# Decayed reads made one head pair ahead, and the norm moved behind the masks, in a bidirectional RWKV-7 kernel

## The chip, the cores and the metric

The kernel runs on one core of a Trainium2 chip. The metric is device time in microseconds, the median of several runs. The engines are PE (TensorE, matmuls), DVE (VectorE), ACT (ScalarE), POOL (GpSimd) and SP (SyncE, which here only issues DMAs). Each engine works through a queue of its own in a fixed order, and waits at an instruction until the semaphores that it needs have been raised.

## What is computed

One layer of a bidirectional RWKV-7 mixer beside a short gated convolution, for 128 context and 256 latent tokens, D = 2048, 32 heads of 64 channels. The input projection `z = h @ w_in` feeds both branches. The first branch is a recurrence in each direction:

```python
def step(S, inp):
    r_t, w_t, k_t, v_t, a_t, b_t = inp
    sa = jnp.einsum('dbhij,dbhj->dbhi', S, a_t)
    S = S * w_t[..., None, :] + sa[..., :, None] * b_t[..., None, :] + v_t[..., :, None] * k_t[..., None, :]
    y = jnp.einsum('dbhij,dbhj->dbhi', S, r_t)
    return S, y
...
y = ys[0] + ys[1]
mu = jnp.mean(y, axis=-1, keepdims=True)
var = jnp.mean(jnp.square(y - mu), axis=-1, keepdims=True)
y = ((y - mu) * lax.rsqrt(var + GN_EPS)).reshape(bsz, t, D_A) * lnx_g + lnx_b
...
y_a = (y.astype(h.dtype) * jax.nn.silu(g_a)) @ w_out_a
...
y_b = (b_gate * u * jax.nn.silu(g_b)) @ w_out_b
merged = jax.nn.sigmoid(m_a) * y_a + jax.nn.sigmoid(m_b) * y_b
return merged @ w_o, S_fin
```

The outputs are the residual streams after a final norm and the final states of the context tokens.

## The kernel before

All data is fp32. A large matmul is made of three passes over operands that are split into a high and a low part (`mm3`, L80 to L83; the split L85 to L89 is a cast on ACT, line L88, and a subtraction on DVE, line L89). Three such matmuls of 128x384 are called a dense step here. The projections are a stream of dense steps (class `Stream`, L111 to L180). The stream loads its weights (`raw`), splits them (`whi`, `wlo`) and is moved on by `ds_.go(n)`: n steps are written into PE's queue at that place. It has an order of fills: rk and gv of the next pair first, then gates (bc, bx, bg, gb, ma, mb), and at the end ob, the output projection of the convolution branch.

The recurrence is worked in chunks of 64 tokens (six, two of context and four of latent tokens) for a pair of heads, in a loop over 16 pairs b (L973 to L1002). One iteration consists of these parts, in the order in which they are written, and PE executes them in this order, with dense steps in between:

- `prep_b` makes the decayed operands: `pr` (kk and r times the decay, the "decayed reads") and `bk` (the keys). Then come 14 dense steps (`PB0`), the transposes of the last pair's normed output (`finish`, py L948), and the masked products pA of direction 0, 6 steps (`PB1`) and of direction 1 (24 small matmuls each, L708). DVE masks them into `A` (L714), SP brings the 32x32 blocks through DRAM into another layout (`ui` L719, `un` L732, `ux` L734), and DVE inverts the triangular systems in 30 short steps (L740, L742), beginning with an add on the diagonal (L745). The result goes back through `uo` and is transposed ("turned").
- `prep_c` brings the transposed v into `sav` by eight POOL DMAs (L777) and transposes the keys (pb L784).
- `prep_a` and `prep_k` make the decay, keys and rates of pair b+1; `prep_k` is called at the fourth step of the scan.
- `scan` runs two chains, 0 over the context chunks and 1 over the latent ones, both directions at once. A chunk is po (reads from the state, L816), an add into sav (L817), pq (L833), a copy, pu (L840), and the new state st (L845). When both chains are done, py2 (L910, 24 small matmuls) makes the outputs and DVE adds them to ytok (L913).
- `norm` (L927 to L942) does mean, variance and scaling of ytok on DVE, with the square on ACT and the power `rs` on POOL (L941).

The order of PE's queue is the order of writing. The orders of the other engines are set by a scheduler at compile time, by priorities: what is written in the scan is raised by 300, and otherwise what is written earlier comes earlier. The function `load_yb` (L511) is called when the stream reaches the first step of ob0. It reads the convolution branch's 16 tiles back from DRAM (`yst_b`, SP), casts them (`ybh`, L508, ACT) and subtracts (`ybl`, L509, DVE).

Of the kernel before, what the change touches and what calls it, by code (L numbers as in the profile page):

```python
# [56 lines left out]
def hybrid_step(ctx, tc, cst, x_prompt, x_sample, state_f, state_b, c, c_ctx, ada_w, ada_b, norm_g,  # L57
# [614 lines left out]
    def prep_b(b, o):  # L672

        r, kk = r_[b], o["kk"]
        o["pr"], o["bk"] = [], []
        for d in range(2):
            ep, em, kd, bn = o["ep"][d], o["em"][d], o["kd"][d], o["bn"][d]
            pr = sp.tile([P, NCH, P], F32, tag=f"pr{d}", name=f"pr_{b}_{d}")
            bk = sp.tile([P, NCH, P], F32, tag=f"bk{d}", name=f"bk_{b}_{d}")
            V.tensor_tensor(bk[:, :, 0:C], c3(bn[:]), c3(em[:]), ALU.mult)  # L680
            V.tensor_tensor(bk[:, :, C:P], c3(kd[:]), c3(em[:]), ALU.mult)
# [20 lines left out]
        for d in range(2):  # L702
# [7 lines left out]
            for n0, w in ((0, 4), (4, 2)):  # L710
                mk = cs[:, m0:m0 + P].rearrange("p (w t) -> p w t", t=C).unsqueeze(1).broadcast_to([P, w, 2, C])
                for h in range(2):
                    f0 = NCH * d + n0
                    last = V.tensor_tensor(A[:, :, f0:f0 + w, hss[h]].rearrange("p w n t -> p n w t"),  # L714
                                           pas[h, n0][:, 0:w, :].rearrange("p n (w t) -> p n w t", t=C), mk,
                                           ALU.mult).ins
# [7 lines left out]
        vt = sp.tile([P, 2, T], F32, tag="vt", name=f"vt_{b}")  # L724
        with tc.issue_after(last):
            for d in range(2):
                V.transpose(vt[:, d], v_[b][:, ::-1] if d else v_[b][:])
# [26 lines left out]
        for d in range(2):  # L754
            box["turned"] = V.transpose(x11[0:32, 12 * d:12 * d + 12, :], blocks(A, d, 0)).ins

    def prep_c(b, o):
# [16 lines left out]
        x = o["vt"][:].rearrange("p d (n e t) -> p (d n) e t", e=2, t=32)  # L774
        for e in range(2):
            for q in range(4):
                G.dma_start(sav[C + 32 * e:C + 32 * e + 32, :, 32 * q:32 * q + 32], x[32 * q:32 * q + 32, :, e, :])  # L777
# [18 lines left out]
    def scan(b, o):  # L796
# [7 lines left out]
        def chain(ch):  # L804
            ls = None
            for i in range((2, 4)[ch]):
# [30 lines left out]
                if need_state:  # L837
# [3 lines left out]
                    for hs in hss:  # L841
                        if zero:
                            V.tensor_copy(st[ch][hs, :, hs], pu[hs, 0:2, hs])
                        else:
                            V.tensor_tensor(st[ch][hs, :, hs], pu[hs, 0:2, hs], ls[hs, :, hs], ALU.add)  # L845
# [81 lines left out]
    def norm(b, o):  # L927
# [4 lines left out]
        V.tensor_reduce(mu[:], y6, AX.X, ALU.add)  # L932
# [251 lines left out]
```

## Time and profile before

| | us |
|---|---|
| median of 3 runs | 2228.72 (2228.09 to 2231.8) |
| the profiled execution | 2230.84 |
| its span in the profile | 2229.1 |
| PE busy | 2168.6 (97%) |
| DVE busy | 1501.9 (67%) |
| ACT busy | 978.4 (44%) |
| POOL busy | 200.9 (9%) |

A profile is of one execution. A row of a group of instructions names the line, the engine, the operation, what is written and read, the shapes and the count; behind the first bar are the busy time in us and the mean of one in ns; behind the second bar is the time that the engine stood idle just before these instructions, and what ended most of it. A row of a timeline begins with the start and the duration in us, and ends with the idle time before it and its releaser in brackets, if there was any. In both, names are without their pair numbers. In the profile, the reader looks for places at which PE, the fullest engine, stands idle, and at what it is waiting for there.

### The profile page before, as it was taken

The page shows a single profiled execution, that of the slowest core. Times are in us where ns is not written, and L with a number is a line of the kernel's source. Part 1 is how long each engine was busy: PE and PEld are TensorE (multiplying, and loading weights), DVE is VectorE, ACT ScalarE, POOL GpSimd, SP SyncE. Part 2 cuts the span into 40 slices and gives each one's busy share as a digit, 9 for nine tenths or more (in the row PEclk, how much of TensorE's full clock was granted, in tenths as well). Part 3 has the DMA queues.
Part 4 walks back from the last instruction along what each step waited for, and adds up shares of the span by engine and source line. Part 5 has one row for each costly group of instructions (what it writes and reads, how often), then busy time and mean ns, then how long its engine had stood idle before and what let it go on. Part 6 is the DMA issues. An engine that isn't in the chain of part 4 may idle for free.

```text
span 2229.1 us, 40796 instructions
## 1 busy us (share of the span) xinstructions
PE 2168.6 (97%) x15924; PEld 2056.5 (92%) x15924; DVE 1501.9 (67%) x3288; ACT 978.4 (44%) x1704; POOL 200.9 (9%) x243
## 2 busy tenths in 40 slices
PE   6999999999999999999999999999999999999998
PEld 3588999999999999999999999999999999898988
DVE  3248567786877777868768786877777775444354
ACT  4245435453535454444436353536353634333333
POOL 2001010101010101111010101010101010000000
PEclk9999999999999999999999999999999999999999
DMA  9975464546464536364554546364546474887633
GB/s 337 346 213 131 142 144 128 126 108 146 107 147 107 133 108 143 112 144 105 138 115 128 126 108 146 108 145 124 138 121 153 147 206 146 292 273 234 219 132 114
DMA packets 480850, 347.88 MB, mean 156 GB/s; under 512 B 134720, under 2 KB 460944, under 8 KB 479760
## 3 DMA queue, kind: packets, MB, share of 16 engines
q1 hardware_dynamic: 475072, 337.20, 54.2%
q0 software_dynamic: 5152, 6.49, 2.0%
q8 instruction: 126, 2.06, 0.4%
q10 hardware_dynamic: 432, 1.57, 0.2%
q14 instruction: 68, 0.56, 0.1%
HBM read 312.09 MB, written 26.21 MB: 152 GB/s over the span
## 4 chain that ended last, share of the span: by engine, by line
PE 72%; DVE 13%; DMA 7%; ACT 3%; issue 2%; SPq 1%; POOL 0%; ACTq 0%; POOLq 0%; DVEq 0%
DMA raw_adah<-in_ada_w_dram 4%; PE d_rk L81 3%; PE d_rk L83 3%; PE d_rk L82 3%; PE d_gv L81 3%; PE d_gv L82 3%; PE d_gv L83 3%; PE pA L708 2%; PE d_oa L81 2%; PE d_oa L83 2%; PE d_oa L82 2%; PE d_bc L81 2%; PE d_mb L81 2%; PE d_gb L81 2%; PE d_mb L82 2%
## 5 line engine op out<-in xcount | busy, mean ns | idle before, releaser
L81 PE MATMUL d_rk<-h_hi,whi_rk 128*128 128x384 f32 x480 | 161.5, 337 | 0.6 <-ACT lst L554 0.6
L81 PE MATMUL d_gv<-h_hi,whi_gv 128*128 128x384 f32 x480 | 161.1, 336 | 0.0
L82 PE MATMUL d_gv<-h_lo,whi_gv 128*128 128x384 f32 x480 | 160.8, 335 | 0.0
L83 PE MATMUL d_gv<-h_hi,wlo_gv 128*128 128x384 f32 x480 | 160.7, 335 | 0.0
L83 PE MATMUL d_rk<-h_hi,wlo_rk 128*128 128x384 f32 x480 | 160.4, 334 | 0.0
L82 PE MATMUL d_rk<-h_lo,whi_rk 128*128 128x384 f32 x480 | 160.4, 334 | 0.0
L740 DVE TENSOR_TENSOR ut<-ux,un 112x30 f32<-112x30 f32 (+7 forms) x480 | 119.3, 248 | 16.6 <-DMA ux<-ui 4.2
L742 DVE TENSOR_TENSOR ux<-ux,ut 112x30 f32<-112x30 f32 (+7 forms) x480 | 119.3, 249 | 13.6
L88 ACT CAST whi_gv<-raw_gv 128x1024 fp32r<-128x1024 f32 (+1 forms) x64 | 64.0, 999 | 139.5 <-PE d_gv L82 34.0
L88 ACT CAST whi_rk<-raw_rk 128x1024 fp32r<-128x1024 f32 x60 | 62.9, 1052 | 119.1 <-PE d_rk L82 37.9
L89 DVE TENSOR_TENSOR wlo_rk<-raw_rk,whi_rk 128x1024 fp32r<-128x1024 f32 x60 | 73.1, 1221 | 50.0 <-ACT whi_rk L88 50.0
L81 PE MATMUL d_ob<-ybh,whi_ob 128*128 128x384 f32 x256 | 88.8, 347 | 3.8 <-ACT whi_ob L88 3.1
L81 PE MATMUL d_bg<-h_hi,whi_bg 128*128 128x384 f32 x256 | 91.8, 359 | 0.0
L81 PE MATMUL d_bc<-h_hi,whi_bc 128*128 128x384 f32 x256 | 91.7, 358 | 0.0
L81 PE MATMUL d_gb<-h_hi,whi_gb 128*128 128x384 f32 x256 | 91.7, 358 | 0.0
L81 PE MATMUL d_bx<-h_hi,whi_bx 128*128 128x384 f32 x256 | 91.5, 358 | 0.0
L81 PE MATMUL d_ma<-h_hi,whi_ma 128*128 128x384 f32 x256 | 91.0, 356 | 0.0
L81 PEld LDWEIGHTS d_rk<-h_hi,whi_rk 128*128 128x128 f32 x480 | 90.1, 188 | 0.9 <-ACT lst L554 0.9
L81 PEld LDWEIGHTS d_gv<-h_hi,whi_gv 128*128 128x128 f32 x480 | 90.4, 188 | 0.2
L82 PEld LDWEIGHTS d_gv<-h_lo,whi_gv 128*128 128x128 f32 x480 | 90.6, 189 | 0.0
L83 PEld LDWEIGHTS d_gv<-h_hi,wlo_gv 128*128 128x128 f32 x480 | 90.5, 188 | 0.0
L81 PE MATMUL d_mb<-h_hi,whi_mb 128*128 128x384 f32 x256 | 90.2, 352 | 0.0
(313 smaller groups left out, 6595.4 us busy)
## 6 DMA issues: line engine op xcount, KB each, us to landing
raw_adah<-in_ada_w_dram SPq DMA_DIRECT2D x64, 512.0 KB, 8.7
raw_rk<-in_w_in_dram SPq DMA_DIRECT2D x60, 512.0 KB, 5.3
raw_gv<-in_w_in_dram SPq DMA_DIRECT2D x60, 512.0 KB, 5.6
raw_ma<-in_w_in_dram SPq DMA_DIRECT2D x16, 1024.0 KB, 5.5
raw_mb<-in_w_in_dram SPq DMA_DIRECT2D x16, 1024.0 KB, 5.5
raw_bc<-in_w_in_dram SPq DMA_DIRECT2D x16, 1024.0 KB, 5.4
raw_bx<-in_w_in_dram SPq DMA_DIRECT2D x16, 1024.0 KB, 5.4
raw_bg<-in_w_in_dram SPq DMA_DIRECT2D x16, 1024.0 KB, 5.5
```

The lines of the kernel that those rows point to most:

```text
L81: TE.matmul(out, wh, xh, start=start, stop=False)
L82: TE.matmul(out, wh, xl, start=False, stop=False)
L83: TE.matmul(out, wl, xh, start=False, stop=stop)
L88: S.copy(hi[0:rows], src)
L89: V.tensor_tensor(lo[0:rows], src, hi[0:rows].bitcast(F32), ALU.subtract)
L708: TE.matmul(pas[h, n // 4 * 4][:, n % 4, :], bk[hss[h], n, :], pr[hss[h], n, :], start=True, stop=True)
L740: V.tensor_tensor(tv, ux[:, 0:m, s:s + 1].broadcast_to([112, m, w]), un[:, s:s + 1, s + 1:].broadcast_to([112, m, w]), ALU.mult)
L742: V.tensor_tensor(ux[:, 0:m, s + 1:], ux[:, 0:m, s + 1:], tv, ALU.add)
```

## The change

- `prep_b` is cut in three. `prep_p` makes bk and is called right behind `prep_k`, in the scan of the pair before. `prep_r` makes pr, in tiles of which there are now two sets (`pr{d}{b % 2}`); it is called in the same scan once chain 0 has written its last state, and its instructions come behind that state.
- The 14 steps and the step behind py2 are no longer written ahead of pA: py2 of pair b-1 and pA of pair b stand directly behind each other on PE. After the loop's first pair, 16 steps stand behind the second pA instead: 6 (`PB1`), and 10 (`NRM`) once the inversion has been written, and only then `finish` of the last pair.
- `norm` of pair b-1 is called behind the masks of pair b, and its first instruction comes behind the last mask.
- The transposed v is in two tiles of another pool, brought to `sav` by 16 half-size POOL DMAs. `ut` shares a buffer with `ns`. The turn of the inverse is written in `prep_a` of the next pair, and the split of `lraw` is written out there.
- `LAST`, the steps added to the window of the last pair, goes from 16 to 30.

```diff
-    PRO, WINDOW, FIRST, LAST = 32, 80, 24, 16
+    PRO, WINDOW, FIRST, LAST, NRM = 32, 80, 24, 30, 10
...
-        with tc.issue_after(box["turned"]) if "turned" in box else ExitStack():
+        if p is not None:
+            with tc.issue_after(lws):
+                p["turn_x"]()
+        with tc.issue_after(box["turned"]) if p is not None else ExitStack():
             box["kn"] = V.tensor_scalar(kn[:], pn, 1e-24, None, ALU.max).ins
...
-    def prep_b(b, o):
+    def prep_p(b, o):
+
+        o["bk"] = [sp.tile([P, NCH, P], F32, tag=f"bk{d}", name=f"bk_{b}_{d}") for d in range(2)]
+        for d in range(2):
+            bk = o["bk"][d]
+            V.tensor_tensor(bk[:, :, 0:C], c3(o["bn"][d][:]), c3(o["em"][d][:]), ALU.mult)
+            V.tensor_tensor(bk[:, :, C:P], c3(o["kd"][d][:]), c3(o["em"][d][:]), ALU.mult)
+
+    def prep_r(b, o):
...
-            pr = sp.tile([P, NCH, P], F32, tag=f"pr{d}", name=f"pr_{b}_{d}")
-            bk = sp.tile([P, NCH, P], F32, tag=f"bk{d}", name=f"bk_{b}_{d}")
-            V.tensor_tensor(bk[:, :, 0:C], c3(bn[:]), c3(em[:]), ALU.mult)
-            V.tensor_tensor(bk[:, :, C:P], c3(kd[:]), c3(em[:]), ALU.mult)
+            pr = sp.tile([P, NCH, P], F32, tag=f"pr{d}{b % 2}", name=f"pr_{b}_{d}")
...
-        yield PB0
+
+    def prep_b(b, o):
...
+            o["masked"] = last
             yield PB1
...
-        vt = sp.tile([P, 2, T], F32, tag="vt", name=f"vt_{b}")
+        vt = [tmp(f"vt_{b}_{d}") for d in range(2)]
...
-        x = o["vt"][:].rearrange("p d (n e t) -> p (d n) e t", e=2, t=32)
-        for e in range(2):
-            for q in range(4):
-                G.dma_start(sav[C + 32 * e:C + 32 * e + 32, :, 32 * q:32 * q + 32], x[32 * q:32 * q + 32, :, e, :])
+        for d in range(2):
+            x = o["vt"][d][:].rearrange("p (n e t) -> p n e t", e=2, t=32)
+            for e in range(2):
+                for q in range(4):
+                    G.dma_start(sav[C + 32 * e:C + 32 * e + 32, NCH * d:NCH * d + NCH, 32 * q:32 * q + 32],
+                                x[32 * q:32 * q + 32, :, e, :])
...
-        yield 1
+        yield 0
         V.tensor_tensor(ytok[:], ytok[:], py[:, 0:3, :], ALU.add)
...
-        V.tensor_reduce(mu[:], y6, AX.X, ALU.add)
+        with tc.issue_after(masked) if masked is not None else ExitStack():
+            V.tensor_reduce(mu[:], y6, AX.X, ALU.add)
...
         pb_gen = prep_b(b, cur)
-        ds_.go(next(pb_gen))
+        for d in range(2):
+            ds_.go(next(pb_gen))
         if prev is not None:
+            norm(b - 1, prev, cur["masked"])
+        drive(pb_gen)
+        n = 0
+        if prev is not None:
+            ds_.go(NRM)
+            n = NRM
             finish(b - 1, prev)
-        drive(pb_gen)
-        n = drive(prep_c(b, cur))
+        n += drive(prep_c(b, cur))
...
             with tc.issue_after(cur["turn"][0]), tc.issue_after(cur["turn"][1]):
                 prep_k(b + 1, nxt)
+                prep_p(b + 1, nxt)
+
+        def reads():
+            with tc.issue_after(cur["st0"]):
+                prep_r(b + 1, nxt)
...
-        drive(scan(b, cur), 300, 3 if b < NB - 1 else None, keys)
-        norm(b, cur)
+        late = ((lambda: all(cur.get("turn", (None,))), keys), (lambda: "st0" in cur, reads))
+        drive(scan(b, cur), 300, late if b < NB - 1 else ())
```

How this moves the instructions is seen at three places. The first is PE, from the end of pair 6's scan into pair 7; names carry the pair's number, and bc4 is a fill of the dense stream. Before:

```order
L910 MATMUL py2_6_9529<-sav_6_8687,A_6_8506 64x64 x24
L81 MATMUL d_bc4_0_9554<-h_hi0_76,whi_bc4_0_0_9447 128x384
L82 MATMUL d_bc4_0_9554<-h_lo0_80,whi_bc4_0_0_9447 128x384
L83 MATMUL d_bc4_0_9554<-h_hi0_76,wlo_bc4_0_0_9448 128x384
L81 MATMUL d_bc4_0_9554<-h_hi0_76,whi_bc4_0_0_9447 128x384
```

And after the change:

```order
L928 MATMUL py2_6_9604<-sav_6_8725,A_6_8482 64x64 x24
L720 MATMUL pA_7_0_0_0_9646<-pr_7_0_9471,bk_7_0_9344 128x128
L720 MATMUL pA_7_0_1_0_9647<-pr_7_0_9471,bk_7_0_9344 128x128
L720 MATMUL pA_7_0_0_0_9646<-pr_7_0_9471,bk_7_0_9344 128x128
L720 MATMUL pA_7_0_1_0_9647<-pr_7_0_9471,bk_7_0_9344 128x128
```

The 15 dense steps that stood between py2 and pA are gone from here. Behind the second pA, where 8 steps stood ahead of pb, there are now 16, py's transposes and 2 more, and 5 further on; the pair has 128 steps as before. Between the first pA and pav, which reads sav ahead of the scan, 110 steps stand where 95 did.

The second place is DVE in the scan of pair 6, in chain 1's second chunk, from behind the add into sav to the new state st1. Before:

```order
L665 TENSOR_TENSOR kd_7_1_9277<-k_7_8882,kd_7_1_9277 128x384
L666 TENSOR_TENSOR sig_7_3_9104<-kn_7_9115,sig_7_3_9104 128x384
L480 TENSOR_TENSOR bu_3_1_8734<-bu_3_1_8734,d_bg3_1_9035 128x384
L89 TENSOR_TENSOR wlo_gb3_1_0_9356<-raw_gb3_1_9353,whi_gb3_1_0_9355 128x1024
L680 TENSOR_TENSOR bk_7_0_9596<-sig_7_2_9092,sig_7_0_9056 128x6x64
L681 TENSOR_TENSOR bk_7_0_9596<-kd_7_0_9269,sig_7_0_9056 128x6x64
L680 TENSOR_TENSOR bk_7_1_9602<-sig_7_3_9104,sig_7_1_9068 128x6x64
L845 TENSOR_TENSOR st0_1144<-pu_6_0_1_9391,ls_6_0_1_9330 64x2x64 x2
L918 STREAM_TRANSPOSE ns_6_9570<-st0_1144 64x64 x4
L681 TENSOR_TENSOR bk_7_1_9602<-kd_7_1_9277,sig_7_1_9068 128x6x64
L845 TENSOR_TENSOR st1_1146<-pu_6_1_1_9402,ls_6_1_1_9346 64x2x64 x2
```

And after the change, behind the same product into kd:

```order
L672 TENSOR_TENSOR sig_7_3_9165<-kn_7_9176,sig_7_3_9165 128x384
L684 TENSOR_TENSOR bk_7_0_9344<-kd_7_0_9332,sig_7_0_9117 128x6x64
L683 TENSOR_TENSOR bk_7_1_9345<-sig_7_3_9165,sig_7_1_9129 128x6x64
L684 TENSOR_TENSOR bk_7_1_9345<-kd_7_1_9340,sig_7_1_9129 128x6x64
L480 TENSOR_TENSOR bu_3_0_8780<-bu_3_0_8780,d_bg3_0_9095 128x384
L480 TENSOR_TENSOR bu_3_1_8809<-bu_3_1_8809,d_bg3_1_9096 128x384
L89 TENSOR_TENSOR wlo_gb3_1_0_9425<-raw_gb3_1_9422,whi_gb3_1_0_9424 128x1024
L805 TENSOR_TENSOR kd_7_0_9332<-kd_7_0_9332,kd_7_1_9340 128x384
L862 TENSOR_TENSOR st0_1144<-pu_6_0_1_9460,ls_6_0_1_9399 64x2x64 x2
L936 STREAM_TRANSPOSE ns_6_9630<-st0_1144 64x64 x4
L693 TENSOR_TENSOR pr_7_0_9471<-kk_7_9081,ep2_1152 128x6x64
L862 TENSOR_TENSOR st1_1146<-pu_6_1_1_9477,ls_6_1_1_9415 64x2x64 x2
```

The first bk has moved ahead of sav; the other bu, the bonus product kd and the first pr have come in ahead of st1.

The third place is pair 15, where load_yb stands in DVE's queue. Before, between the masks of direction 0:

```order
L714 TENSOR_TENSOR A_15_18861<-pA_15_0_0_0_18862,cs_74 128x4x2x64
L714 TENSOR_TENSOR A_15_18861<-pA_15_0_1_0_18863,cs_74 128x4x2x64
L509 TENSOR_TENSOR ybl0_18892<-yst_b_0_18896,ybh0_18888 128x384
L509 TENSOR_TENSOR ybl0_18892<-yst_b_1_18900,ybh0_18888 128x384
L440 TENSOR_TENSOR ga_15_18885<-ga_15_18885,d_gv15_0_18746 128x384
```

And after the change, far behind the masks:

```order
L440 TENSOR_TENSOR ga_15_19114<-ga_15_19114,d_gv15_0_18930 128x384
L758 TENSOR_SCALAR ux_1159<-ux_1159 48x16
L753 TENSOR_TENSOR ut_15_19033<-ux_1159,un_1158 112x30
L755 TENSOR_TENSOR ux_1159<-ux_1159,ut_15_19033 112x30
L753 TENSOR_TENSOR ut_15_19033<-ux_1159,un_1158 112x29
L755 TENSOR_TENSOR ux_1159<-ux_1159,ut_15_19033 112x29
L753 TENSOR_TENSOR ut_15_19033<-ux_1159,un_1158 112x56
L755 TENSOR_TENSOR ux_1159<-ux_1159,ut_15_19033 112x2x28
L509 TENSOR_TENSOR ybl0_19121<-yst_b_0_19125,ybh0_19117 128x384
L753 TENSOR_TENSOR ut_15_19033<-ux_1159,un_1158 112x54
```

The first ybl now stands behind the diagonal add on ux and six steps of the inversion. On SP, the loads yst_b likewise stand behind the transfers of ux.

More of the change, by code (lines that the diff above doesn't have):

```diff
@@ L611, in hybrid_step, with prep_a @@
     G.memset(ux[:], 0.0)
-    def prep_a(b, o):
+    def prep_a(b, o, p=None):
         bs = slice(b * P, (b + 1) * P)
@@ L627, in prep_a @@
                 with tc.issue_after(box["kn"]) if m == 0 and "kn" in box else ExitStack():
-                    lwh, lwl = split(lraw[:], [96, 2, P], "lwh", "lwl", sp, f"{b}_{m}", rows=96)
+                    lwh = sp.tile([96, 2, P], F32R, tag="lwh", name=f"lwh_{b}_{m}")
+                    lwl = sp.tile([96, 2, P], F32R, tag="lwl", name=f"lwl_{b}_{m}")
+                    S.copy(lwh[:], lraw[:])
+                    lws = V.tensor_tensor(lwl[:], lraw[:], lwh[:].bitcast(F32), ALU.subtract).ins
                 yield 2
@@ L722, in prep_b @@
             G.tensor_tensor(o["bk"][d][:], o["bk"][d][:], o["ep"][d][:, :, C:C + 1].broadcast_to([P, NCH, P]), ALU.mult)
-        vt = sp.tile([P, 2, T], F32, tag="vt", name=f"vt_{b}")
+        vt = [tmp(f"vt_{b}_{d}") for d in range(2)]
         with tc.issue_after(last):
             for d in range(2):
-                V.transpose(vt[:, d], v_[b][:, ::-1] if d else v_[b][:])
+                V.transpose(vt[d][:], v_[b][:, ::-1] if d else v_[b][:])
         o["vt"] = vt
@@ L735, in prep_b @@
                               ui[:].rearrange("d e i (m g) t -> (d e i) m g t", g=2)[:, :, g, :])
-        ut = sp.tile([112, 128], F32, tag="ut", name=f"ut_{b}")
+        ut = sp.tile([P, 2, C], F32, tag="ns", name=f"ut_{b}")[0:112].rearrange("p a b -> p (a b)")
         for s in range(1, 31):
@@ L752, in prep_b, with turn @@
                 nc.sync.dma_start(blocks(A, d, e), uo[d, e].rearrange("i s t -> s i t"))
-        for d in range(2):
-            box["turned"] = V.transpose(x11[0:32, 12 * d:12 * d + 12, :], blocks(A, d, 0)).ins
+        def turn():
+            for d in range(2):
+                box["turned"] = V.transpose(x11[0:32, 12 * d:12 * d + 12, :], blocks(A, d, 0)).ins
+        o["turn_x"] = turn
     def prep_c(b, o):
@@ L844, in chain @@
                         else:
-                            V.tensor_tensor(st[ch][hs, :, hs], pu[hs, 0:2, hs], ls[hs, :, hs], ALU.add)
+                            x = V.tensor_tensor(st[ch][hs, :, hs], pu[hs, 0:2, hs], ls[hs, :, hs], ALU.add)
+                            o[f"st{ch}"] = x.ins
                     yield 0
@@ L925, in scan, with norm @@
                                       nst[p0:p0 + 32, d, :].rearrange("i (b j) -> i b j", j=32))
-    def norm(b, o):
+    def norm(b, o, masked=None):
         ytok = o["ytok"]
@@ L953, in finish, with drive @@
         nc.sync.dma_start(ya_d[b], ya[:])
-    def drive(gen, prio=0, at=None, fn=None):
-        n = i = 0
+    def drive(gen, prio=0, late=()):
+        n = 0
+        late = list(late)
         while True:
-            if i == at:
-                fn()
-            i += 1
+            for x in [x for x in late if x[0]()]:
+                x[1]()
+                late.remove(x)
             with tc.high_priority(offset=prio):
@@ L963, in drive @@
             if u is None:
+                assert not late
                 return n
@@ L971, in hybrid_step @@
     prep_k(0, cur)
+    prep_p(0, cur)
+    prep_r(0, cur)
+    ds_.go(PB0)
     prev = None
@@ L979, in hybrid_step @@
         pb_gen = prep_b(b, cur)
-        ds_.go(next(pb_gen))
+        for d in range(2):
+            ds_.go(next(pb_gen))
         if prev is not None:
+            norm(b - 1, prev, cur["masked"])
+        drive(pb_gen)
+        n = 0
+        if prev is not None:
+            ds_.go(NRM)
+            n = NRM
             finish(b - 1, prev)
-        drive(pb_gen)
-        n = drive(prep_c(b, cur))
+        n += drive(prep_c(b, cur))
         nxt = {}
+        w = WINDOW + (FIRST if b == 0 else LAST if b == NB - 1 else 0)
         if b < NB - 1:
@@ L989, in hybrid_step @@
                 n += 1
-            n += drive(prep_a(b + 1, nxt))
-        w = WINDOW + (FIRST if b == 0 else LAST if b == NB - 1 else 0)
+            n += drive(prep_a(b + 1, nxt, cur))
+        else:
+            cur["turn_x"]()
         if n < w:
@@ L998, in keys @@
                 prep_k(b + 1, nxt)
-        drive(scan(b, cur), 300, 3 if b < NB - 1 else None, keys)
-        norm(b, cur)
+                prep_p(b + 1, nxt)
[4 more added lines that the diff above has]
+        drive(scan(b, cur), 300, late if b < NB - 1 else ())
         prev, cur = cur, nxt
+    norm(NB - 1, prev)
     ds_.go(12)
```

5 lines of the change are left out of this document (2 added, 3 removed).

## The prediction

> **What bounds the kernel now.** The page comes first, for the question which engine is full. Its head and its first part:
>
> ```profile
> span 2229.1 us, 40796 instructions
> PE 2168.6 (97%) x15924; PEld 2056.5 (92%) x15924; DVE 1501.9 (67%) x3288; ACT 978.4 (44%) x1704; POOL 200.9 (9%) x243
> ```
>
> PE works 97% of the span, so a change of order alone can win only what PE stands idle, 60 us, and much of that lies before and behind the loop. One steady iteration of the head-pair loop, by windows (from the first pA burst of pair 7 to that of pair 8; the columns are length, then busy time and count for PE, PEld, DVE, ACT, POOL):
>
> ```profile
> 938.40:1042.70 104.30, 103.52 (x814) 101.24 (x813) 79.95 (x187) 46.86 (x86) 11.01 (x12) 1.00 0.50 122
> ```
>
> PE idles 0.8 us of 104.3 here, at the full granted clock (1.00). The change leaves the number of matmuls and of dense steps per iteration as it is (128 steps of three 128x384 matmuls; only their places differ). A step costs 0.52 us: these two rows of PE's timeline are the same matmul of two successive steps.
>
> ```profile
> 1782.55 0.33 PE L81 MATMUL d_ob<-ybh,whi_ob 128*128 128x384 f32 x1
> 1783.07 0.33 PE L81 MATMUL d_ob<-ybh,whi_ob 128*128 128x384 f32 x1
> ```
>
> So everything hangs on PE's waits. The groups of instructions, with the idle time ahead of them and its releaser behind the last bar, show where they are near the changed code:
>
> ```profile
> L816 PE MATMUL po<-st,pr 128*128 128x128 f32 x320 | 49.5, 277 | 7.8 <-DVE st L845 7.8
> L708 PE MATMUL pA<-pr,bk 64*128 64x128 f32 x768 | 52.0, 281 | 2.0 <-DVE pr L685 1.2 <-DVE A L714 0.8
> L682 DVE TENSOR_TENSOR pr<-kk,ep 128x384 f32<-128x384 f32 x32 | 17.7, 553 | 20.6 <-PE po L816 20.6
> ```
>
> The masked product pA waits 2.0 us in the whole run, the scan's po 7.8 us, always for the state st that DVE writes. Those 9.8 us are the most that this region can give back. The third row is the wait that the second pr buffer removes: DVE stands 20.6 us in front of pr, but PE does not wait for DVE in that time.
>
> **The scan.** What the wait of po is made of is seen in pair 6, first PE, then DVE:
>
> ```profile
> 912.04 0.60 PE L840 MATMUL pu<-sav,bt 128*128 128x128 f32 x4
> 915.48 0.68 PE L816 MATMUL po<-st,pr 128*128 128x128 f32 x4 [0.72 <-DVE st L845]
> ```
>
> ```profile
> 908.47 0.41 DVE L817 TENSOR_TENSOR sav<-po,sav 64x256 f32<-64x256 f32 x1
> 910.20 1.21 DVE L89 TENSOR_TENSOR wlo_gb<-raw_gb,whi_gb 128x1024 fp32r<-128x1024 f32 x1
> 911.34 0.54 DVE L680 TENSOR_TENSOR bk<-sig,sig 128x384 f32<-128x384 f32 x1
> 911.81 0.54 DVE L681 TENSOR_TENSOR bk<-kd,sig 128x384 f32<-128x384 f32 x1
> 914.75 0.59 DVE L845 TENSOR_TENSOR st<-pu,ls 64x128 f32<-64x128 f32 x2
> ```
>
> pu is finished at 912.6, but DVE comes to st only at 914.75, because it has no gap from sav (908.47) on: 6.28 us of queued work. One 128x384 product takes 0.47 us of the queue (911.34 to 911.81). Between the same sav and the same st, seven such products stand before the change (kd, sig, bu and four bk) and nine after it (kd's bonus product, the second bu and the first pr come in, one bk goes out to an earlier place). That is 2 x 0.47 = 0.94 us more of queue, and PE's wait grows from 0.72 to about 1.66 us in pairs 2, 6 and 10: **+2.8**. The same count over the other fills of the dense stream: pairs 3, 7 and 11 get 0.42 more ahead of this st and a new wait of about 0.7 at the following sav (+3.4 in three); pairs 4 and 8 lose 0.1 each; pairs 5 and 9 lose a wait of about 0.5 each, since pr no longer stands there; pairs 12 to 14 stay under the point at which PE waits. Sum **+5.0 us**. From below it is bounded by -7.8 (all waits of po gone), from above by +8 (0.94 in each of pairs 2, 3, 4, 6, 7, 8, 10 and 11). I take the count.
>
> The pr products themselves cost nothing new: they are done several dense steps ahead of py2, so the 14 steps that hid them before are not missed by the first pA. The eight further vt transfers are POOL's:
>
> ```profile
> L777 POOL DMA_DIRECT2D sav<-vt x128 | 79.2, 626 | 32.1 <-ACT whi_rk L88 16.7 <-DVE lo_bs L605 8.2 <-DVE vt L727 4.3
> ```
>
> 16 x 0.626 = 10.0 us in place of 5.0, hidden behind the 110 dense steps (57 us) that now lie between the first pA and pav, which reads sav. Those were 95 steps, so the chain from masks through inversion to turn gets 15 x 0.52 = 7.8 us more cover; PE did not wait for it, so nothing is gained.
>
> **The norm behind the masks.** These rows are masks and norm of pair 7's turn into pair 8:
>
> ```profile
> 1035.79 0.55 DVE L932 TENSOR_REDUCE mu<-ytok 128x6 f32<-128x384 f32 x1
> 1038.65 1.35 POOL L941 TENSOR_TENSOR rs<-var,nhalf 128x6 f32<-128x6 f32 x1 [41.54 <-DVE var L939]
> 1040.03 0.56 DVE L942 TENSOR_TENSOR ytok<-ytok,rs 128x384 f32<-128x384 f32 x1 [1.53 <-POOL rs L941]
> 1042.75 1.61 PE L708 MATMUL pA<-pr,bk 64*128 64x128 f32 x24
> 1047.63 1.61 PE L708 MATMUL pA<-pr,bk 64*128 64x128 f32 x24
> 1048.82 1.95 DVE L714 TENSOR_TENSOR A<-pA,cs 128x512 f32<-128x512 f32 x4 [0.77 <-PE pA L708]
> ```
>
> The second pA starts 4.88 after the first, its masks end 1050.77, 8.0 after the first. The norm from mu to ytok took 4.8 us (1035.79 to 1040.59); behind the masks one weight split, one transpose of vt and one POOL issue are put into it, about 1.5 us. So ytok is ready about 14.3 us after the first pA. PE comes to its transposes after the second pA (4.88 + 1.61 = 6.5) and 16 steps (8.3), at 14.8. It costs **0**, but the cover is only half a microsecond.
>
> **The last pair.** Here the order moves against PE. In pair 15 the filler changes from gv15 to ob0, and ob0's first step calls load_yb: 16 loads yst_b on SP, 16 casts ybh on ACT, 16 subtractions ybl on DVE. Since 14 steps moved behind the masks, this call is now written behind the inversion: SP issues yst_b behind ux, and DVE reaches ybl behind the diagonal add on ux, which waits for ux to land, and six steps of the inversion. What these take, from pair 15 before:
>
> ```profile
> 1789.33 1.34 DVE L714 TENSOR_TENSOR A<-pA,cs 128x512 f32<-128x512 f32 x3
> 1802.17 0.18 DVE L745 TENSOR_SCALAR ux<-ux 48x16 f32<-48x16 f32 x1 [1.15 <-DMA ux<-ui]
> 1805.10 0.18 DVE L740 TENSOR_TENSOR ut<-ux,un 112x30 f32<-112x30 f32 x1
> 1805.99 0.22 DVE L740 TENSOR_TENSOR ut<-ux,un 112x56 f32<-112x56 f32 x1
> L509 DVE TENSOR_TENSOR ybl<-yst_b,ybh 128x384 fp32r<-128x384 f32 x16 | 9.4, 634 | 0.3 <-ACT ybh L508 0.3
> ```
>
> From the last mask (1790.67) to the add on ux 11.5 us; six steps take about 1.3; one ybl 0.6. With the masks at 8.0, the first ybl is ready at 8.0 + 11.5 + 0.2 + 1.3 + 0.6 = 21.6 us. PE is through the second pA and its 10 steps of gv15 at 6.5 + 5.2 = 11.7 and needs ybl in the second matmul of ob0, at 11.9: a wait of 9.7 us. There is no other work in PE's queue. It replaces these waits of before:
>
> ```profile
> 1776.03 0.44 PE L81 MATMUL d_ob<-ybh,whi_ob 128*128 128x384 f32 x1 [0.71 <-ACT ybh L508]
> 1776.77 0.45 PE L82 MATMUL d_ob<-ybl,whi_ob 128*128 128x384 f32 x1 [0.30 <-DVE ybl L509]
> 1779.31 0.45 PE L82 MATMUL d_ob<-ybl,whi_ob 128*128 128x384 f32 x1 [0.34 <-DVE ybl L509]
> 1790.06 0.44 PE L784 MATMUL pb<-cs,bk 128*128 128x128 f32 x2 [0.78 <-DVE A L714]
> ```
>
> together 2.1. Net 7.6, **+7.5**. The way of ux, and of the equally large transfer back (KB each, median us from issue to landing):
>
> ```profile
> ui<-A SPq DMA_DIRECT2D x64, 48.0 KB, 1.8
> ux<-ui SPq DMA_DIRECT2D x32, 96.0 KB, 8.3
> uo<-ux SPq DMA_DIRECT2D x32, 96.0 KB, 2.9
> ```
>
> ux is late because its own transfer takes 8.3. From below the term is +2 (ux landing in the 2.9 of uo, 5.4 sooner), from above +10 (none of the old waits goes). [...]
>
> **The end.** Behind the last scan stand these two waits:
>
> ```profile
> 1884.31 0.52 PE L948 MATMUL py<-cs,ytok 128*128 128x128 f32 x3 [0.23 <-DVE ytok L942]
> 1914.94 0.45 PE L81 MATMUL d_ob<-ybh,whi_ob 128*128 128x384 f32 x1 [3.06 <-ACT whi_ob L88]
> ```
>
> The last py has 12 steps ahead of it in place of 13, and waits 0.5 more; the first step of ob7 has two steps more between, and waits up to 1.0 less: -0.5, between -1 and +0.5.
>
>  **Sum: 5.0 + 7.5 - 0.5 = +12.0 us.** The profiled execution took 2230.84 (span 2229.1 and 1.7 around it) and would become 2242.8; it lies 2.1 above the median 2228.72, so the median becomes **2240.7**.
>
> **Rivals.** *Faster, 2219:* the freed DVE runs ahead. 20.6 us of standing in front of pr are gone, and if this pulls every st ahead of its po, the 7.8 and the 2.0 go, and 2228.7 - 9.8 = 2219, provided that load_yb is early enough. For it: DVE is only 67% busy. Against it: the waits come from work ahead of st, and more of it stands there now. *No change, 2229:* the scan keeps its 7.8 or gains what pair 15 loses; PE is as full as before, and steps were only moved. For it speaks the equal number of steps. *Slower still, 2253:* the norm overruns its half microsecond. Its price is seen in pair 1, with the group of that product:
>
> ```profile
> 306.44 1.28 DVE L952 TENSOR_TENSOR ya<-ya,ga 128x384 f32<-128x384 f32 x1
> 305.83 1.48 POOL L722 TENSOR_TENSOR bk<-bk,ep 128x768 f32<-128x768 f32 x1 [5.22 <-PE pA L708]
> L952 DVE TENSOR_TENSOR ya<-ya,ga 128x384 f32<-128x384 f32 x16 | 9.6, 598 | 0.1
> ```
>
> A product of DVE that takes 0.55 in the other 15 ((9.6 - 1.28) / 15) took 1.28, until just behind POOL's end at 307.31. POOL's second bk product follows the second pA directly and ends near 8.0, where the norm now begins; if it slips into the norm's subtraction, the chain gets up to 1.48 longer, 0.9 beyond the cover, in 14 pairs: 13 us, 2240.7 + 12.6 = 2253. [...]
>
> **Chances.** Forecast 0.5 (own range 2232 to 2248), norm late 0.12, no change 0.2, faster 0.18. About 0.2%, 4.5 us, is what a measurement of this kernel can tell from nothing. So faster 0.18, same 0.2, slower 0.62. The range takes in most of both rivals: 2222 to 2254.
>
> **What the profile after would show.** Right: po's idle time behind st rises from 7.8 to 12 or 13 us; d_ob waits some 9 us for ybl or ybh around the first ob0 step, with yst_b issued behind ux; py's transposes of ytok do not wait; DVE's 20.6 in front of pr is gone. Wrong: po's idle time falls; ob0 begins without a long wait; or PE waits for ytok in every pair, which is the slower rival.

## The result, and the profile after

The changed kernel takes **2247.06 us** (median of 4 runs, 2245.36 to 2248.92); the kernel before, run beside it, 2230.22. The ratio is 1.0076, interval 1.0059 to 1.0094, or 16.8 us slower. Forecast were 2240.7 and 12.0 us slower: the side was right, the size five microseconds short, and the way to it only half right. The profiled execution took 2245.36. Its head, and the busy times of the engines:

```profile
span 2243.6 us, 41132 instructions
PE 2168.0 (97%) x15924; PEld 2064.8 (92%) x15924; DVE 1497.4 (67%) x3288; ACT 978.0 (44%) x1704; POOL 263.4 (12%) x371
```

PE is as busy as before (2168.6) and the span is 14.5 longer, so PE stands idle more. The groups show where; these are PE's rows that changed, and DVE's pr:

```profile
L81 PE MATMUL d_bg<-h_hi,whi_bg 128*128 128x384 f32 x256 | 93.1, 364 | 6.0 <-DVE bc L467 6.0
L81 PE MATMUL d_gb<-h_hi,whi_gb 128*128 128x384 f32 x256 | 92.8, 362 | 6.0 <-DVE bu L480 6.0
L81 PE MATMUL d_bc<-h_hi,whi_bc 128*128 128x384 f32 x256 | 91.9, 359 | 2.2 <-DVE bg L486 2.2
L81 PE MATMUL d_ob<-ybh,whi_ob 128*128 128x384 f32 x256 | 89.4, 349 | 10.2 <-ACT ybh L508 8.2 <-DVE smb L521 2.0
L720 PE MATMUL pA<-pr,bk 64*128 64x128 f32 x768 | 52.8, 285 | 2.0 <-DVE pr L696 2.0
L833 PE MATMUL po<-st,pr 128*128 128x128 f32 x320 | 49.0, 275 | 2.5 <-DVE st L862 2.5
L693 DVE TENSOR_TENSOR pr<-kk,ep 128x384 f32<-128x384 f32 x32 | 17.8, 555 | 0.4
```

Three things are read from them. The last row: the wait that the second buffer was to remove is gone, 20.6 us before and 0.4 now. The row of po: its wait **fell**, 7.8 to 2.5, where the prediction had it rise. And the first three rows: dense steps wait 14.2 us in all, a wait that the kernel before has nowhere. One of these waits stands in each of pairs 2, 3, 5, 6, 7, 9, 10 and 11. Here is the one of pair 6, first PE:

```profile
908.54 0.42 PE L81 MATMUL d_gb<-h_hi,whi_gb 128*128 128x384 f32 x1
...
911.17 0.60 PE L850 MATMUL pq<-sav,A 128*128 128x128 f32 x4
913.78 0.44 PE L81 MATMUL d_gb<-h_hi,whi_gb 128*128 128x384 f32 x1 [2.01 <-DVE bu L480]
```

and DVE at the same time:

```profile
910.05 0.54 DVE L683 TENSOR_TENSOR bk<-sig,sig 128x384 f32<-128x384 f32 x1
...
911.78 0.55 DVE L684 TENSOR_TENSOR bk<-kd,sig 128x384 f32<-128x384 f32 x1
912.25 0.55 DVE L683 TENSOR_TENSOR bk<-sig,sig 128x384 f32<-128x384 f32 x1
912.72 0.55 DVE L684 TENSOR_TENSOR bk<-kd,sig 128x384 f32<-128x384 f32 x1
913.19 1.01 DVE L480 TENSOR_TENSOR bu<-bu,d_bg 128x384 f32<-128x384 f32 x2
```

A fill of two column blocks sums four steps into one PSUM accumulator and then turns to the next. There are three accumulators (pool `pd`, `bufs=3`). The fill gb took the free one for its first four steps (908.54 on); for the fifth it needs one of the two that hold the finished d_bg, and these are emptied by `bu` (L480). In the kernel before, the first of the two products ended at 908.55, and PE came to the fifth step of gb at 909.40 without a wait (DVE, PE, DVE):

```profile
908.01 0.54 DVE L480 TENSOR_TENSOR bu<-bu,d_bg 128x384 f32<-128x384 f32 x1
909.40 0.42 PE L81 MATMUL d_gb<-h_hi,whi_gb 128*128 128x384 f32 x1
909.74 0.54 DVE L480 TENSOR_TENSOR bu<-bu,d_bg 128x384 f32<-128x384 f32 x1
```

The margin was 0.85 us. In DVE's queue of the changed kernel all four products bk stand ahead of bu. I call this an **accumulator wait**. By windows from the first pA of one pair to that of the next, here pairs 6 and 7 (columns as in the prediction's view; the column behind POOL is the granted clock):

```profile
828.06:933.27 105.21, 103.20 (x818) 101.37 (x814) 80.40 (x190) 48.20 (x87) 14.69 (x20) 1.00 0.48 120
933.27:1040.06 106.79, 104.78 (x818) 102.95 (x814) 81.48 (x190) 46.74 (x86) 14.89 (x20) 0.98 0.49 123
```

Both pairs hold one accumulator wait of 2.01, yet pair 7 takes 1.58 more, and all of it is PE's busy time (104.78 against 103.20) for the same count of matmuls. Windows behind the wait of pair 6, behind that of pair 7 and behind the long wait in pair 15, and one of the kernel before behind its wait of 3.06 ahead of ob7, show why:

```profile
913.40:917.40 4.00, 3.62 (x24) 3.62 (x24) 3.87 (x11) 0.89 (x1) 0.00 (x0) 1.00 0.00 0
1018.60:1022.60 4.00, 3.60 (x14) 3.61 (x15) 2.90 (x7) 1.13 (x2) 0.00 (x0) 0.60 0.00 0
1794.90:1800.90 6.00, 5.78 (x17) 5.38 (x18) 3.48 (x12) 2.05 (x4) 3.30 (x6) 0.50 0.66 172
1914.90:1920.90 6.00, 5.32 (x20) 4.94 (x21) 5.98 (x9) 4.15 (x7) 0.00 (x0) 0.72 0.59 174
```

The granted clock (third number from the end) fell behind some of these waits, to 0.60, 0.50 and 0.72 against 1.00 in the first row, and matmuls followed each other in 0.32 us in place of 0.17 until it was back. After four of the six long accumulator waits (pairs 2, 7, 10, 11) it fell, after two it did not.

In pair 15 the wait before ob0 came as predicted, here on PE, ACT, SP and DVE:

```profile
1794.90 0.69 PE L81 MATMUL d_ob<-ybh,whi_ob 128*128 128x384 f32 x1 [8.17 <-ACT ybh L508]
1795.81 0.69 PE L82 MATMUL d_ob<-ybl,whi_ob 128*128 128x384 f32 x1 [0.22 <-DVE ybl L509]
```

```profile
1794.34 1.12 ACT L508 CAST ybh<-yst_b 128x384 fp32r<-128x384 f32 x2 [5.52 <-DMA yst_b<-yb_d]
1788.80 1.27 SPq L747 DMA_DIRECT2D ux<-ui  x2
1790.37 11.92 SPq L507 DMA_DIRECT2D yst_b<-yb_d  x10
1793.23 0.17 DVE L758 TENSOR_SCALAR ux<-ux 48x16 f32<-48x16 f32 x1 [1.27 <-DMA ux<-ui]
```

SP's queue carries yst_b behind ux, so the cast got its data at 1794.34; DVE, behind the add on ux and six steps, added only 0.22.

The span splits at the first pA of pairs 0, 1 and 15 (starts from PE's timeline; 15 dense steps, 7.8 us, have moved from ahead of a pair's first pA to behind it, so that only the pairs between compare directly):

| us | before | after | difference | without the moved steps |
|---|---|---|---|---|
| to pair 0's first pA | 185.36 | 186.52 | +1.2 | +1.2 |
| pair 0 | 118.67 | 110.14 | -8.5 | -0.7 |
| pairs 1 to 14 | 1468.97 | 1478.19 | +9.2 | +9.2 |
| pair 15 and the rest | 456.1 | 468.75 | +12.6 | +4.8 |

### The profile page after: what moved, and what is told of

Its sections match the earlier page's. It is cut to its first block, busy times and chain, and to the rows that moved or that the text cites. A ratio compares the mean times of both kernels' runs of the same rounds, so it can differ in the third digit from the quotient of the medians.

```text
span 2243.6 us, 41132 instructions
## 1 busy us (share of the span) xinstructions
PE 2168.0 (97%) x15924; PEld 2064.8 (92%) x15924; DVE 1497.4 (67%) x3288; ACT 978.0 (44%) x1704; POOL 263.4 (12%) x371
## 4 chain that ended last, share of the span: by engine, by line
PE 78%; DVE 10%; DMA 5%; ACT 3%; issue 2%; SPq 1%; POOL 0%; DVEq 0%; POOLq 0%; ACTq 0%
PE d_rk L81 4%; PE d_rk L83 4%; PE d_rk L82 4%; PE d_gv L81 4%; PE d_gv L83 4%; PE d_gv L82 4%; DMA raw_adah<-in_ada_w_dram 3%; PE pA L720 2%; PE d_oa L81 2%; PE d_oa L83 2%; PE d_oa L82 2%; PE d_gb L81 2%; PE d_bc L81 2%; PE d_mb L81 2%; PE d_gb L83 2%
## 5 line engine op out<-in xcount | busy, mean ns | idle before, releaser
L793 POOL DMA_DIRECT2D sav<-vt x256 | 144.4, 571 | 96.1 <-DVE vt L740 53.6
L735 POOL TENSOR_TENSOR bk<-bk,ep 128x768 f32<-128x768 f32 x32 | 50.2, 1569 | 690.1 <-PE pA L720 639.3
L893 POOL MEMSET A<- 64x1536 f32 x16 | 22.0, 1377 | 685.1 <-issue 576.0
```

The lines of the kernel that those rows point to most:

```text
L735: G.tensor_tensor(o["bk"][d][:], o["bk"][d][:], o["ep"][d][:, :, C:C + 1].broadcast_to([P, NCH, P]), ALU.mult)
L793: G.dma_start(sav[C + 32 * e:C + 32 * e + 32, NCH * d:NCH * d + NCH, 32 * q:32 * q + 32], x[32 * q:32 * q + 32, :, e, :])
L893: G.memset(A[C:P, 0, :, :], 0.0)
```

## The experiments

Two parts of the change could be to blame for the accumulator waits: the products bk, which now come with the keys, or pr with its second buffer, which now comes in the scan. Against both stands the reading of the prediction, that DVE simply has more queue ahead of st. For pair 15 the question was whether the place of load_yb is the cause, or the DMA traffic that pair 15 has anyway.

**e1_yb.** In pair 15 the ten dense steps in which ob0 begins, and so load_yb, are written ahead of the inversion again; PE's order stays.

```diff
             norm(b - 1, prev, cur["masked"])
+        if b == NB - 1:
+            ds_.go(NRM)
         drive(pb_gen)
...
-            ds_.go(NRM)
+            if b < NB - 1:
+                ds_.go(NRM)
```

> The changed kernel, but in pair 15 the ten steps behind the second pA are written ahead of the inversion, so that load_yb comes ahead of it on SP and DVE; PE's own order is the same. If the place of load_yb is the cause of the 8.2 us wait of ob0, that wait falls to 2 to 5 us (the first ybl now stands behind the norm only) and the time by 3 to 6, to about 2242. If it is the way of the yb tiles themselves (loads, casts), the wait stays near 8 and the time at 2247.

Measured: 2236.62, ratio 1.0045 (1.0027 to 1.0063). The wait for ybh is 3.03 in place of 8.17, with 0.96 for ybl; the accumulator waits stay (6.0, 6.0, 2.2). From pair 15's first pA to the end it is 462.6 us in place of 468.75: the place of load_yb costs some 6 us. Each time with the kernel before run beside it, the loss falls from 16.8 to 8.4 us, more than the 3 to 6 of the forecast; what goes beyond the 6 is not explained by the edit alone. In the profiled execution pairs 1 to 14 are 3.2 shorter at the same waits; the granted clock falls behind two of the six long ones (to 0.63 and 0.58 over four microseconds) where it fell behind four.

**e2_bk.** The products bk are released behind chain 0's last state (st0), with pr, and no longer with the keys.

```diff
                 prep_k(b + 1, nxt)
-                prep_p(b + 1, nxt)
...
             with tc.issue_after(cur["st0"]):
+                prep_p(b + 1, nxt)
                 prep_r(b + 1, nxt)
```

> The changed kernel, but the bk products are called with the pr products, behind chain 0's last state, and not with the keys. Theory A (bk stands ahead of the products bc, bu and bg that empty PE's accumulators, and PE waits for a free accumulator): the waits of d_gb, d_bg and d_bc, 14.2 us in eight pairs, fall under 2 and the time by 12 to 14, to 2233 to 2235. Rival C (pr in the scan does it): they stay, 2247. Rival D (the lengthened queue ahead of st, as forecast): the waits of po go from 2.5 to under 2 and the others stay, 2246.

Measured: 2235.72, ratio 1.0036 (1.0022 to 1.005). The accumulator waits are gone, as theory A has it, and po waits 9.0, of which the expectation says nothing:

```profile
L81 PE MATMUL d_gb<-h_hi,whi_gb 128*128 128x384 f32 x256 | 91.8, 359 | 0.0
L833 PE MATMUL po<-st,pr 128*128 128x128 f32 x320 | 49.9, 278 | 9.0 <-DVE st L862 8.8
```

Pairs 1 to 14 take 1466.5, against 1478.2 in the changed kernel and 1469.0 before: the accumulator waits and the fallen clock behind them, less what they save at po, cost some 12 us. What is left against before stands behind pair 15's first pA (ob0 waits 7.0).

**e3_prio.** The operations that empty an accumulator are raised in priority by 300, as those of the scan are; bk stays with the keys.

```diff
-                                    consume(i, ps[i])
+                                    with tc.high_priority(offset=300):
+                                        consume(i, ps[i])
```

> The changed kernel with bk where it is, but every operation that empties an accumulator of the dense stream is raised to the scan's priority. Theory A: the 14.2 us of d_gb, d_bg and d_bc fall under 2, as when bk is moved, and the time goes to 2233 to 2237; up to 3 us may come back as waits of po, since bk still stands ahead of st. Rivals C and D: no gain, 2245 to 2250.

Measured: 2241.01, ratio 1.006 (1.0045 to 1.0075). This is above the forecast of 2233 to 2237. The accumulator waits are gone here too, and the wait of po is back, by more than the 3 us expected:

```profile
L834 PE MATMUL po<-st,pr 128*128 128x128 f32 x320 | 50.0, 279 | 8.2 <-DVE st L863 6.9 <-DVE ns L937 1.2
```

Pairs 1 to 14 take 1471.6. It is the place in DVE's queue that counts, not DVE's amount of work, which is the same. The end is worse (475.1 from pair 15's first pA to the end, 7.5 at ob0 and 3.1 at ob7 among it, the latter as in the kernel before); here everything that `consume` calls was raised, not the emptying alone, and which of it costs this was not tried.

**b_bk.** The other way round: the kernel before, and of the change only bk with the keys.

```diff
+    def prep_p(b, o):
+        o["bk"] = [sp.tile([P, NCH, P], F32, tag=f"bk{d}", name=f"bk_{b}_{d}") for d in range(2)]
...
                 prep_k(b + 1, nxt)
+                prep_p(b + 1, nxt)
```

> The kernel before, with the bk products alone called in the scan with the keys (pr in one buffer, the 14 steps and the norm where they were). Theory A: the accumulator waits of 2.0 us appear in pairs 2, 3, 6, 7, 10 and 11 and about 1 us in 5 and 9, 14 us in all, less some 4 us of po waits: 2238 to 2244. Rival C: no such waits, 2229 to 2231.

Measured: 2234.27, ratio 1.0036 (1.0023 to 1.005), below the forecast of 2238 to 2244. The accumulator waits arise from this edit alone, and po's wait falls alone with it:

```profile
L81 PE MATMUL d_gb<-h_hi,whi_gb 128*128 128x384 f32 x256 | 93.0, 363 | 6.2 <-DVE bu L480 6.2
L81 PE MATMUL d_bg<-h_hi,whi_bg 128*128 128x384 f32 x256 | 92.5, 361 | 6.1 <-DVE bc L467 6.1
L820 PE MATMUL po<-st,pr 128*128 128x128 f32 x320 | 48.7, 274 | 2.7 <-DVE st L849 2.7
```

Pairs 1 to 14 take 1479.0 in the profiled execution, as in the changed kernel; this execution, at 2239.35, is the slowest of five, and the granted clock fell behind three of its six long waits (to 0.58, 0.68 and 0.57 over four microseconds).

**b_pr.** The kernel before, and of the change only the second pr buffer, pr in the scan and the split of vt into two tiles with 16 transfers.

```diff
-            pr = sp.tile([P, NCH, P], F32, tag=f"pr{d}", name=f"pr_{b}_{d}")
+            pr = sp.tile([P, NCH, P], F32, tag=f"pr{d}{b % 2}", name=f"pr_{b}_{d}")
...
-        vt = sp.tile([P, 2, T], F32, tag="vt", name=f"vt_{b}")
+        vt = [tmp(f"vt_{b}_{d}") for d in range(2)]
...
+        def reads():
+            with tc.issue_after(cur["st0"]):
+                prep_r(b + 1, nxt)
```

> The kernel before, with pr alone made in the scan in two buffers, and v in two tiles of the other pool with 16 POOL transfers (both need the space); bk, the 14 steps, the norm and the turn stay. Theory A (only bk's place blocks the accumulators): no wait of d_gb, d_bg or d_bc over 0.3 us; the time stays between 2225 and 2233. Rival C: waits of d_gb, d_bg and d_bc, 2235 and up. The old rival of a freed DVE: the po waits of 7.8 us fall by over 5 and the time to about 2223.

Measured: 2227.98, ratio 1.0008 (0.9998 to 1.0017): no change. There is no accumulator wait, and po waits 8.1:

```profile
L824 PE MATMUL po<-st,pr 128*128 128x128 f32 x320 | 49.8, 278 | 8.1 <-DVE st L853 8.1
```

So the title part of the change, the reads in a second buffer, is worth nothing here by itself: DVE's 20.6 us in front of pr were idle time that nobody waited for.

**g1_prio_yb.** The changed kernel with both causes mended: only the three products that read the accumulators (bc, bu, bg) are raised, and in pair 15 ten steps are written ahead of the norm, and 16 more ahead of the transposes of ytok.

```diff
-        V.tensor_tensor(u[:], u[:], ps, ALU.mult)
+        with tc.high_priority(offset=300):
+            V.tensor_tensor(u[:], u[:], ps, ALU.mult)
...
+            if b == NB - 1:
+                ds_.go(NRM)
             norm(b - 1, prev, cur["masked"])
...
-            ds_.go(NRM)
-            n = NRM
+            w = 16 if b == NB - 1 else NRM
+            ds_.go(w)
+            n = w + (NRM if b == NB - 1 else 0)
```

> The changed kernel with the scan's priority for the three DVE products alone that read a dense accumulator (bc, bu, bg), and in pair 15 ten steps, with load_yb, ahead of the norm and of the inversion, and 16 more ahead of py's transposes. Theory A: accumulator waits under 2 us in all (14.2 without the edit), po waits up to 8; ob0 waits under 3 us (8.2, and 3.0 + 1.0 with the ten steps behind the norm). Sum from the changed kernel: -14 + 6 - 7 = 2232. If ob0 waits on the transfers of the yb tiles, it keeps 4 us, and 2234.

**g2_late.** The same in pair 15, without priorities; bk and pr are released behind chain 1's second new state.

```diff
-            with tc.issue_after(cur["st0"]):
+            with tc.issue_after(cur["sts"][1]):
+                prep_p(b + 1, nxt)
                 prep_r(b + 1, nxt)
```

> The changed kernel with pair 15 as in g1_prio_yb, and bk and pr both released behind chain 1's second state instead of chain 0's last; no raised priorities. Theory A: no accumulator waits, since bc, bu and bg come first again. The po wait for the second state goes too (seven products fewer ahead of it), and what is late next is the third state, with six products ahead of it: 0.3 to 0.8 us in some pairs. 2226 to 2231.

**g3_later.** As g2_late, but pr is released behind chain 1's third state.

```diff
+        def keys2():
+            with tc.issue_after(cur["sts"][1]):
                 prep_p(b + 1, nxt)
...
-            with tc.issue_after(cur["st0"]):
+            with tc.issue_after(cur["sts"][2]):
                 prep_r(b + 1, nxt)
```

> As g2_late, but pr is released only behind chain 1's third state. Theory A: no accumulator waits, po waits under 4 us in all, since four products fewer stand ahead of the third state than in g2_late; pr is made some 5 us before pA needs it, so pA does not wait. 2222 to 2227, which would be faster than the kernel before. If pr comes too late, pA waits by 1 us or more in most pairs, and the time is 2235 or more.

Measured, of the three:

| | us | ratio | accumulator waits | po | ob0 at its start | py of ytok, pairs 15 and 9 |
|---|---|---|---|---|---|---|
| g1_prio_yb | 2226.19 | 1.0000 (0.999 to 1.0009) | 0 | 5.1 | 0 | 3.83, 1.39 |
| g2_late | 2226.64 | 1.0000 (0.999 to 1.0009) | 0 | 9.3 | 0 | 5.72, 1.40 |
| g3_later | 2221.3 | 0.9978 (0.9969 to 0.9987) | 0 | 4.0 | 0 | 4.49, 1.40 |

With both causes taken away the loss is gone, in two different ways (g1 and g2). The first came out 6 us below its forecast. What is gained at ob0 returns in part as a new wait: with ob0's first steps early, PE comes to pair 15's transposes of ytok before the norm is done. With bk and pr released in one place (g2) po waits 9.3, with the two spread over two places (g3) 4.0, and the time falls by as much, 5.3 us.

**g4_py.** As g3_later, with 13 steps in place of 10 (`NRM`) ahead of those transposes, and 26 in place of 16 in pair 15.

```diff
-    PRO, WINDOW, FIRST, LAST, NRM = 32, 80, 24, 30, 10
+    PRO, WINDOW, FIRST, LAST, NRM = 32, 80, 24, 30, 13
...
-            w = 16 if b == NB - 1 else NRM
+            w = 26 if b == NB - 1 else NRM
```

> As g3_later, with 13 steps in place of 10 ahead of py's transposes in pairs 1 to 14 and 26 in place of 16 in pair 15. In g3_later py waits 1.40 us in pair 9 and 4.49 in pair 15, and the norm's cover is 0.35 us in the others. Three steps are 1.56 us, ten are 5.2: both waits should go and nothing else should move: 5.9 us less, 2215 to 2217, 0.995 of the kernel before. If the wait only changes its place (to pb behind the later bk, or to ob0), the time stays at 2219 to 2222.

Measured: **2213.91** (2213.11 to 2215.8), ratio 0.9938 (0.9925 to 0.9952), faster than both kernels. Its head, its rows of po and of ob0:

```profile
span 2211.3 us, 41110 instructions
PE 2158.8 (98%) x15924; PEld 2053.7 (93%) x15924; DVE 1495.0 (68%) x3288; ACT 977.3 (44%) x1704; POOL 262.6 (12%) x371
L833 PE MATMUL po<-st,pr 128*128 128x128 f32 x320 | 49.2, 276 | 4.0 <-DVE st L862 4.0
L81 PE MATMUL d_ob<-ybh,whi_ob 128*128 128x384 f32 x256 | 88.1, 344 | 1.7 <-DVE smb L521 1.0 <-ACT whi_ob L88 0.7
```

The two waits at py are gone, 5.9 us, and the median is 7.4 lower (8.8, if each is taken against the kernel before that ran beside it). PE's busy time fell too (2162.6 in g3): behind g3's wait of 4.49 the granted clock was 0.51 for six microseconds. The mean clock of the profiled execution is 0.995 in g3 and 0.996 here.

**after_again.** The changed kernel once more.

> The changed kernel itself, beside the best one on one chip. The accumulator waits, the ob0 wait and the wait of py in pair 9 are in the order of the program, so they return in the same pairs with the same lengths within 0.1 us: d_gb, d_bg and d_bc 14 us, d_ob 8 at its first step, py 1.4; ratio to the kernel before 1.006 to 1.009.

Measured: 2245.69, ratio 1.0081 (1.0067 to 1.0095), with the same accumulator waits in the same pairs (6.0, 6.0, 2.1), py's 1.39 in pair 9, and the clock falling behind the same four accumulator waits (to 0.57, 0.57, 0.66 and 0.57 over four microseconds). What follows pair 15's first pA did not repeat so closely: ob0 waits 7.16 in place of 8.17, and later steps of ob wait 4.8 in place of 2.0, so that this part takes 472.85 us in place of 468.75.

## Why the prediction was right in sign and short in size

**The scan (forecast +5.0): the step that failed.** The prediction counted the products between sav and st in DVE's queue, took each as 0.47 us more ahead of st, and had po's waits grow from 7.8 to 12 or 13. They fell to 2.5. The order it quotes holds the cause: behind the change "the other bu" comes in ahead of st1, and all of bk stands ahead of both bu. That was read as more queue for st; what it meant is that bu, which empties an accumulator of the dense stream, comes later. PE stands on the accumulator, so it comes to po later, and st is ready by then: the old wait at po is not removed but swallowed by an earlier and longer one. b_bk shows that bk's place alone does it, e2_bk and e3_prio that it goes with bk's place or with bu's. In pairs 1 to 14 PE's idle time rose by 8.4 us (9.7 to 18.0): 14.2 of accumulator waits and 1.4 in pair 9 (below) came in, 7.3 of older waits went, most of them po's. The fallen clock adds four times 1.6. That makes 14.8, and the pairs grew by 9.2; of the 5.6 between, py2 and pA in one burst give 0.17 a pair by PE's timeline, 2.4 in all, and the rest stays open. The prediction named a fall of po's idle time as a sign that it is wrong, and this sign came. That its term still has the right side is luck: the loss arose at another place, which the count did not look at.

**The last pair (forecast +7.5): the mechanism was right.** ob0 waits because load_yb is written behind the inversion. Forecast was a wait of 9.7, and measured were 8.17 and 0.22; the one that came last was the cast behind the late yst_b, which the prediction named beside ybl. So the price, worked out along DVE's way to ybl, came near by way of another instruction: both stand behind ux. In place of 2.1 of old waits this is +6.3. What the forecast left out is the clock: for the six microseconds behind this wait it was 0.50, and 17 matmuls came 0.32 us apart in place of 0.17, some 2.5 us more. A later wait of 1.53 for smb, the product that empties ob's accumulators, came in too. e1_yb moves that place alone and gets back 6.1 of the span behind pair 15's first pA. One thing in this step of the prediction is weaker than it reads. It puts the 8.3 us of ux down to ux's own transfer. But un, twice as large (192 KB, 6.1 us to landing in the changed kernel, where ux takes 6.6), is issued on SP's queue just ahead of ux, in pair 15 at 1787.97 and 1788.80, so a wait behind un is not ruled out.

**The end (forecast -0.5): not settled.** In the two profiled executions the wait of 3.06 ahead of ob7 and the 0.64 behind it went to 0.47, and that of the last py, 0.23, to nothing: -3.5. The fallen clock behind the old wait went with it (0.72 over six microseconds before, from 1914.90 on, 1.00 in the changed kernel from 1933.00 on). So pair 15 and the rest come to +4.8 in all. But the waits at ob7 differ between runs that have the same order there. The changed kernel, in the two executions:

```profile
1933.99 0.44 PE L81 MATMUL d_ob<-ybh,whi_ob 128*128 128x384 f32 x1 [0.47 <-DVE smb L521]
```

```profile
1932.81 0.45 PE L81 MATMUL d_ob<-ybh,whi_ob 128*128 128x384 f32 x1 [0.37 <-ACT whi_ob L88]
1937.08 0.45 PE L81 MATMUL d_ob<-ybh,whi_ob 128*128 128x384 f32 x1 [0.99 <-DVE smb L521]
```

And b_pr, which keeps the order of the kernel before there:

```profile
1912.50 0.44 PE L81 MATMUL d_ob<-ybh,whi_ob 128*128 128x384 f32 x1 [0.70 <-ACT whi_ob L88]
1916.77 0.44 PE L81 MATMUL d_ob<-ybh,whi_ob 128*128 128x384 f32 x1 [0.99 <-DVE smb L521]
```

Between the two rows of after_again stands another wait of 0.64, between those of b_pr one of 0.65. So the 3.06 of the kernel before does not come each time, and how much of the -3.5 is due to the change is not shown; in after_again pair 15 and the rest come to +8.9.

**The norm behind the masks (forecast 0): right, with the numbers forecast.** Pair 7's turn, on PE and DVE:

```profile
933.27 1.61 PE L720 MATMUL pA<-pr,bk 64*128 64x128 f32 x24
947.20 0.56 DVE L961 TENSOR_TENSOR ytok<-ytok,rs 128x384 f32<-128x384 f32 x1 [2.05 <-POOL rs L960]
948.11 0.49 PE L967 MATMUL py<-cs,ytok 128*128 128x128 f32 x3
```

ytok is ready 14.49 after the first pA (forecast 14.3), PE comes to it at 14.84 (14.8). The cover of half a microsecond held in all pairs but pair 9, where PE waited 1.40. The slower rival, by which POOL's product slips onto the norm in 14 pairs, did not occur.

**pr and vt (forecast 0): right**, by b_pr, for the two alone; together with the norm behind the masks, a late transfer of vt costs the 1.40 in pair 9 (below). The rival *faster* (a freed DVE that pulls every st ahead of its po) is refuted by the same run, in which po still waits 8.1. The sum: 12.0 was forecast, 14.5 measured between the profiled executions and 16.8 between the medians, with the scan and the clock as the missing parts and, in that execution, the end against them.

## What to carry to other kernels

An instruction that empties a PSUM accumulator is a release, not only work (here bc, bu and bg, for which dense steps waited 14.2 us): when something is moved in a queue, ask of each instruction that it is moved past which buffer that one frees, and how many steps the producer has until it needs it. A wait that vanishes at one place (po, 7.8 to 2.5) may have been swallowed by an earlier one, so look at the sum over the engine and not at the row. And price a wait of the engine that bounds the kernel at more than its length: here the granted clock fell to 0.57 to 0.68 behind four of the six waits of 2.01, and each fall cost about 1.6 us on top.
